# A 3x3 convolution with 2x2 max pooling: the load of the weights is issued by ScalarE instead of SyncE

## The chip, the core and the metric

The kernel runs on one core of a Trainium2 chip. The metric is the device time of one execution in microseconds (us). The kernel before takes 101.24 us, the median of three runs (100.98 to 101.30).

## What is computed

The reference, cut to its core:

```python
# x: (16, 64, 64, 64) f32, weight: (128, 64, 3, 3) f32, zero padding of 1
conv[b, co] += weight[co, ci, kh, kw] * x_pad[b, ci, kh:kh+h, kw:kw+w]   # over ci, kh, kw
output[b, c, i, j] = max(conv[b, c, 2*i:2*i+2, 2*j:2*j+2])               # 2x2 max pooling
```

## The kernel before

**Tiling.** Two images are worked on together: their 2 x 64 input channels fill the 128 partitions, so there are 8 pairs p. A pair is cut into 4 strips of 16 rows, which makes 32 strips s. A strip has two halves h, one for each image, and each half is a matmul stream with 64 rows of the array (two streams, one in each half of the array, run beside each other). The input of pair p stands as bf16 in `xb[p]`. Matmuls (L248, in `product`) read `xb` or sums and differences of its rows (`sum`, `dif`, `skip`, made by `rows_op`, L278) and add up in the eight PSUM banks `acc`. ScalarE takes results out of the banks (L287, L293, L295, L309), VectorE makes the two maxima (L300, L322), and stores to DRAM go out on SyncE's queue (L317).

**The weights.** They are loaded once, as 128 partitions (output channels) x 576 floats, into the tile `wraw` (L105, L106). Nothing can be multiplied before they have been through a chain. ScalarE and VectorE make seven bf16 blocks `wq` out of them: G0, G1, G2 are the three kernel rows (cast on ScalarE, L173), D0, D2, GM and GP are differences and sums of these (on VectorE, L181, by way of `gsum`), and each block gets a copy of its first column group behind its last one (L141, L143). TensorE turns each block with three transposes (L155), and ScalarE and VectorE bring the turned blocks out of PSUM into `wt` (L165, L169), which L248 uses as its weights.

**The first rows.** `HEAD_LOADS` (L39) names six loads of f32 rows into `xf`, issued right behind the weights' load by the loop at L107 through `load` (L89): of pair 0 the rows 0 to 17 (the upper bound is not included), 17 to 33, 33 to 49 and 49 to 64, and of pair 1 the rows 0 to 17 and 17 to 33. They are cast to `xb` by VectorE or ScalarE (L100, in `cast_rows`). All later rows are loaded and cast by GpSimd's DMA queue (L94, in `cload`); the first of them waits for the cast of rows 49 to 64 of pair 0.

**What sets the order.** The schedule is manual. The string `ORDER` lists the work as tokens, and each engine works in the order of its own tokens: `D0`, `GS`, `D2`, `GM`, `GP` are VectorE's weight blocks, `g0a`, `g1a`, `g2a` ScalarE's, `u...` the copies of a column group, `T...` the transposes, `V...` the copies out of PSUM, `CV.p.lo.hi` and `CA.p.lo.hi` the casts of rows on VectorE and ScalarE, `S`, `E`, `D` the sums, differences and skips of rows. SyncE's and ScalarE's DMA issues stand in the order of the code. Ahead of `ORDER`, eight matmuls of ones (L393) keep TensorE at work while the weights come.

Of the kernel before, what the change touches and what calls it, by code (L numbers as in the profile page):

```python
# [10 lines left out]
def kernel(  # L11
# [7 lines left out]
    nc = tc.nc  # L19
# [83 lines left out]
        made_by[f"C.{p}.{lo}.{hi}"] = inst  # L103

    wraw = const.tile([CO, CI * K * K], FP32)  # L105
    nc.sync.dma_start(out=wraw, in_=weight.rearrange("a b c d -> a (b c d)"))  # L106
    for rows in HEAD_LOADS:  # L107
        load(*rows)
    ident = const.tile([128, 128], BF16)
# [358 lines left out]
```

## Time and profile before

| | |
|---|---|
| median of three runs | 101.24 us |
| the profiled execution, its own time | 101.24 us |
| its span (first to last instruction) | 99.4 us |
| busy: TensorE matmuls | 94.3 us (95%) |
| busy: VectorE | 88.0 us (88%) |
| busy: ScalarE | 87.8 us (88%) |
| busy: GpSimd | 58.5 us (59%) |
| moved by DMA | 18.81 MB |

Times in the views count from the start of the span. PE is TensorE's matmuls, PEld its weight loads, DVE is VectorE, ACT ScalarE, POOL GpSimd and SP SyncE; a q behind a name is that engine's instruction queue, on which it issues DMAs. The DMA queue q1 is that of SyncE, q10 that of ScalarE and q0 that of GpSimd. An arrow in square brackets names what the engine was waiting for.

### The profile page before, as it was taken

What the parts mean: (1) busy time and instruction counts of PE and PEld (TensorE: products, weight loads), DVE (VectorE), ACT (ScalarE), POOL (GpSimd) and SP (SyncE); (2) the same over time, 40 slices, a digit from 0 to 9 for tenths busy, and PEclk for the clock granted to TensorE, in tenths of its full rate; (3) what the DMA queues carried; (4) which work ended last, traced back from release to release, by engine and by line L of the source; (5) the groups of instructions that cost most, each with busy time, mean ns of one, the idle gap of its engine ahead of it and who ended that gap; (6) DMA issues with size and microseconds to landing.
All of it is one profiled execution on the core that took longest, in us unless ns stands there. A gap on an engine that the chain in (4) does not pass through costs nothing.

```text
span 99.4 us, 2421 instructions
## 1 busy us (share of the span) xinstructions
PE 94.3 (95%) x857; PEld 63.5 (64%) x857; DVE 88.0 (88%) x178; ACT 87.8 (88%) x196; POOL 58.5 (59%) x55
## 2 busy tenths in 40 slices
PE   6999999999999999999999999999999999999930
PEld 2368445577678755566677777777777777746400
DVE  0599999999999999999999889989989998967970
ACT  5599998999999998998987999999989899999850
POOL 7000897299957947299179998774594399300000
PEclk9999999999999999999999999999999999999999
DMA  2999769999999999999995057898943107333144
GB/s 44 287 352 412 309 86 196 198 160 298 226 217 226 231 231 226 251 255 294 238 308 170 6 178 242 106 220 102 250 163 127 53 7 254 115 113 102 38 141 138
DMA packets 11740, 18.81 MB, mean 189 GB/s; under 512 B 976, under 2 KB 9168, under 8 KB 11728
## 3 DMA queue, kind: packets, MB, share of 16 engines
q0 software_dynamic: 1872, 6.80, 37.5%
q1 hardware_dynamic: 9712, 11.73, 35.7%
q8 instruction: 6, 0.10, 0.4%
q10 hardware_dynamic: 144, 0.13, 0.4%
q14 instruction: 6, 0.05, 0.2%
HBM read 17.07 MB, written 8.39 MB: 256 GB/s over the span
## 4 chain that ended last, share of the span: by engine, by line
PE 82%; DVE 6%; DMA 6%; SPq 1%; issue 0%; ACT 0%; DVEq 0%
PE acc L248 82%; DMA xf<-in_x_dram 6%; DVE acc L300 3%; DVE xb L100 1%; DVE xf L322 1%; DVE skip L278 1%; DVE dif L278 0%; SPq L89 0%; ACT od L309 0%; SPq L106 0%; DVE sum L278 0%; DVEq L463 0%; DVEq L300 0%
## 5 line engine op out<-in xcount | busy, mean ns | idle before, releaser
L248 PE MATMUL acc<-skip,wt_G 64*128 64x504 bf16 (+1 forms) x312 | 64.2, 377 | 0.1
L248 PEld LDWEIGHTS <-wt_G 64*128 64x128 bf16 x432 | 36.8, 94 | 16.3 <-issue 2.0
L300 DVE TENSOR_TENSOR acc<-acc,ev 128x512 f32<-128x512 f32 x64 | 43.1, 693 | 3.0 <-ACT ev L293 1.2
L278 POOL TENSOR_TENSOR skip<-xb 128x1024 bf16<-128x1024 bf16 x18 | 38.0, 2126 | 11.5 <-PE acc L248 2.8
L248 PE MATMUL acc<-dif,wt_GM 64*128 64x512 bf16 (+1 forms) x156 | 39.9, 376 | 0.0
L248 PE MATMUL acc<-sum,wt_GP 64*128 64x512 bf16 (+1 forms) x156 | 37.2, 377 | 0.2 <-DVE acc L300 0.2
L287 ACT COPY acc<-acc 128x512 f32<-128x512 f32 x52 | 30.5, 586 | 2.8 <-PE acc L248 0.9
L293 ACT ACTIVATE ev<-acc 128x512 f32<-128x512 f32 x52 | 31.5, 610 | 1.3 <-PE acc L248 1.0
L309 ACT COPY od<-acc 128x256 f32<-128x256 f32 x64 | 23.0, 382 | 1.5 <-PE acc L248 1.2
L248 PE MATMUL acc<-xb,wt_G 64*128 64x504 bf16 (+7 forms) x84 | 17.5, 340 | 0.0
L248 PEld LDWEIGHTS <-wt_GP 64*128 64x128 bf16 x156 | 14.2, 94 | 5.1 <-issue 0.6
L248 PE MATMUL acc<-xb,wt_D 64*128 64x504 bf16 (+3 forms) x84 | 17.3, 346 | 0.0
L248 PEld LDWEIGHTS <-wt_GM 64*128 64x128 bf16 x156 | 14.4, 94 | 3.8 <-issue 0.5
L322 DVE TENSOR_TENSOR xf<-acc,od 128x256 f32<-128x256 f32 x32 | 12.7, 417 | 1.1 <-ACT od L309 1.0
L278 POOL TENSOR_TENSOR sum<-xb 128x512 bf16<-128x512 bf16 x6 | 6.9, 1150 | 10.9 <-DVE skip L278 7.9
L322 DVE TENSOR_TENSOR o<-acc,od 128x256 f32<-128x256 f32 x32 | 12.7, 416 | 0.6 <-ACT od L309 0.2
L248 PE MATMUL acc<-sum,wt_G 64*128 64x504 bf16 (+1 forms) x36 | 9.6, 377 | 0.0
L278 DVE TENSOR_TENSOR sum<-xb 128x1024 bf16<-128x1024 bf16 (+1 forms) x16 | 9.3, 589 | 0.0
L248 PEld LDWEIGHTS <-wt_D 64*128 64x128 bf16 x84 | 7.0, 94 | 2.0
L94 POOL DMA_DIRECT2D xb<-in_x_dram x13 | 7.8, 602 | 0.0
L278 DVE TENSOR_TENSOR dif<-xb 128x1024 bf16<-128x1024 bf16 (+1 forms) x12 | 7.7, 644 | 0.0
L295 ACT COPY ev<-acc 128x512 f32<-128x512 f32 x12 | 7.1, 604 | 0.0
(38 smaller groups left out, 36.9 us busy)
## 6 DMA issues: line engine op xcount, KB each, us to landing
out_dram<-o SPq DMA_DIRECT2D x15, 256.0 KB, 6.9
xb<-in_x_dram POOLq DMA_DIRECT2D x7, 496.0 KB, 9.3
xb<-in_x_dram POOLq DMA_DIRECT2D x6, 528.0 KB, 8.0
out_dram<-xf SPq DMA_DIRECT2D x8, 256.0 KB, 6.8
out_dram<-xf SPq DMA_DIRECT2D x15, 128.0 KB, 1.9
xf<-in_x_dram SPq DMA_DIRECT2D x3, 512.0 KB, 6.7
xf<-in_x_dram SPq DMA_DIRECT2D x2, 544.0 KB, 6.7
xf<-in_x_dram SPq DMA_DIRECT2D x1, 480.0 KB, 7.4
```

The lines of the kernel that those rows point to most:

```text
L94: inst = nc.gpsimd.dma_start(out=xb[p][:, lo + 1 : hi + 1, :], in_=rows_of(p, lo, hi))
L100: inst = nc.scalar.copy(out=dst, in_=src) if engine == "A" else nc.vector.tensor_copy(out=dst, in_=src)
L248: nc.tensor.matmul(t[:, i0:i1, o0:o1], wt[block][lo : lo + CI, tap_of(block, kw, h), :], rows(lo, i0, i1, c0, c1), start=start and kw == 1 ...
L278: inst = engine.tensor_tensor(out=dst, in0=in0, in1=in1, op=op)
L287: nc.scalar.copy(out=acc[home("B", part, s, h)][:, span, :], in_=acc[home("A", part, s, h)][:, span, :])
L293: nc.scalar.mul(dst, src, -1.0)
L295: nc.scalar.copy(out=dst, in_=src)
L300: nc.vector.tensor_tensor(out=t, in0=t, in1=ev[s % NEV, h][:, span, :], op=MAX)
L309: nc.scalar.copy(out=od[s % NEV, h][:, span, :], in_=acc[home("B", part, s, h)][:, span, 1::2])
L322: nc.vector.tensor_tensor(out=ot[s % len(ot)][:, h, i0:i1, :], in0=t[:, :, 0::2], in1=od[s % NEV, h][:, i0:i1, :], op=MAX)
```

## The change

The load of the weights is issued by ScalarE. Nothing else is changed in the code:

```diff
     wraw = const.tile([CO, CI * K * K], FP32)
-    nc.sync.dma_start(out=wraw, in_=weight.rearrange("a b c d -> a (b c d)"))
+    nc.scalar.dma_start(out=wraw, in_=weight.rearrange("a b c d -> a (b c d)"))
     for rows in HEAD_LOADS:
         load(*rows)
```

Two engines have another program by it. On SyncE, at the start of the program, the rows before, and behind them the rows now, are these (`wraw` is the tile of the weights, `xf_79` and `xf_80` the f32 rows of pairs 0 and 1):

```order
0 L463 UNCONDITIONAL_BRANCH
1 L106 DMA wraw<-in_weight_dram 128x576
2 L89 DMA xf_79<-in_x_dram 128x1088
3 L89 DMA xf_79<-in_x_dram 128x1024 x2
4 L89 DMA xf_79<-in_x_dram 128x960
5 L89 DMA xf_80<-in_x_dram 128x1088
6 L89 DMA xf_80<-in_x_dram 128x1024
```

```order
0 L463 UNCONDITIONAL_BRANCH
1 L89 DMA xf_79<-in_x_dram 128x1088
2 L89 DMA xf_79<-in_x_dram 128x1024 x2
3 L89 DMA xf_79<-in_x_dram 128x960
4 L89 DMA xf_80<-in_x_dram 128x1088
5 L89 DMA xf_80<-in_x_dram 128x1024
6 L317 DMA out_dram<-o_113 128x2x256
```

The weights' load has left SyncE's queue, and each of the six row loads has moved up one place; the load of rows 0 to 17 is now the first.

On ScalarE, also at the start, the program now begins like this:

```order
0 L463 UNCONDITIONAL_BRANCH
1 L106 DMA wraw<-in_weight_dram 128x576
2 L173 ACT_TABLE_LOAD
3 L173 CAST wq_G_142<-wraw 128x192
4 L141 COPY wq_G_142<-wq_G_142 128x64
5 L173 CAST wq_G_144<-wraw 128x192
6 L173 CAST wq_G_143<-wraw 128x192
```

The weights' load stands ahead of the table load, which was the first instruction before; the rest of ScalarE's 199 instructions follow in the same order, and the programs of TensorE, VectorE and GpSimd are the same as before.

## The prediction

> **What bounds the kernel now.** I read the chain of waits first, in order of time, because it names what the end hangs on:
>
> ```profile
> 0.74 0.37 SPq L106
> 1.11 0.06 issue
> 1.17 0.42 SPq L89
> 1.59 0.05 issue
> 1.64 5.93 DMA xf<-in_x_dram
> 7.57 0.02 issue
> 7.59 0.70 DVE xb L100
> ...
> 9.69 0.61 DVE skip L278
> 10.30 0.05 issue
> 10.35 81.31 PE acc L248 x744
> ```
>
> From 10.35 us on TensorE works through 744 matmuls in 81.31 us without a break that the chain would put down to anything else. Whatever moves the point 10.35 moves the end by as much, unless that long run has slack in it, and the chain shows none. So the question is what sets 10.35. The chain says: the landing of rows 17 to 33 at 7.57 (the second load of rows), and behind it VectorE. The change touches two instructions of this chain, the issues at 0.74 and at 1.17, and read by itself it promises rows 0.42 us earlier.
>
> But a chain shows only what ended last, not by how much. So I looked at VectorE's own rows before 7.59:
>
> ```profile
> 3.65 0.50 DVE L181 TENSOR_TENSOR wq_D<-wraw 128x192 bf16<-128x192 f32 x1 [3.65 <-DMA wraw<-in_weight_dram]
> 4.07 0.50 DVE L181 TENSOR_TENSOR gsum<-wraw 128x192 f32<-128x192 f32 x1
> ...
> 5.61 0.50 DVE L181 TENSOR_TENSOR wq_GP<-gsum,wraw 128x192 bf16<-128x192 f32 x1
> 6.03 0.35 DVE L169 COPY wt_D<-acc 128x384 bf16<-128x384 bf16 x1
> 6.29 0.45 DVE L100 CAST xb<-xf 128x576 bf16<-128x576 f32 x1
> 6.66 0.35 DVE L169 COPY wt_G<-acc 128x384 bf16<-128x384 bf16 x1
> 7.04 0.42 DVE L278 TENSOR_TENSOR sum<-xb 128x512 bf16<-128x512 bf16 x1
> 7.59 0.69 DVE L100 CAST xb<-xf 128x1024 bf16<-128x1024 f32 x1
> ```
>
> VectorE starts at 3.65, when the weights have landed, and from there each row starts before the one ahead of it has ended (the first at 3.65 lasts 0.50 and the next starts at 4.07), until 7.04 + 0.42 = 7.46. Only from 7.46 to 7.59 does it stand still for the rows: **0.13 us**. So there are two paths that reach 7.59 nearly together. One is the rows. The other is the weights' landing and 3.81 us of VectorE behind it (7.46 - 3.65). Rows that come earlier are worth 0.13 us at most. Weights that come later cost all of their delay but 0.13 us.
>
> The DMA issues, looked at in the first 3 and the first 2 us, and the use of the DMA engines between the landings:
>
> ```profile
> q1 hardware_dynamic: 129, 0.30, 43.8%
> ...
> wraw<-in_weight_dram SPq DMA_DIRECT2D x1, 288.0 KB, 2.9
> ```
>
> ```profile
> xf<-in_x_dram SPq DMA_DIRECT2D x1, 544.0 KB, 5.1
> xf<-in_x_dram SPq DMA_DIRECT2D x1, 512.0 KB, 5.9
> ```
>
> ```profile
> 0.74:1.74 1.00, 0.96 (x3) 0.43 (x4) 0.00 (x0) 1.00 (x1) 0.93 (x6) 1.00 0.00 0
> 1.74:3.63 1.89, 1.89 (x6) 0.59 (x4) 0.00 (x0) 0.28 (x1) 0.74 (x6) 1.00 1.02 276
> 3.63:6.25 2.62, 2.61 (x22) 1.22 (x20) 2.60 (x9) 2.42 (x8) 0.00 (x0) 1.00 0.99 297
> 6.25:7.57 1.32, 1.21 (x20) 0.98 (x21) 1.18 (x4) 1.32 (x5) 0.00 (x0) 1.00 0.96 338
> 7.57:8.85 1.28, 1.28 (x28) 1.15 (x24) 1.22 (x3) 1.28 (x4) 0.00 (x0) 1.00 0.99 402
> ```
>
> The last two columns are the busy share of the 16 DMA engines and GB/s. The weights land 2.9 us after their issue at 0.74, at 3.64. Rows 0 to 17 land 5.1 us after theirs at 1.17, at 6.27. Nothing moves until 1.74, and from there to 8.85 the DMA engines are busy all the time (0.96 to 1.02). So the queue is no place where an earlier issue finds idle DMA engines: the first packet moved 1.0 us after the first issue, and the rows that were issued second were already standing behind the weights when these were through. The 129 packets of 0.30 MB are 2.3 KB each, one per partition (576 floats of 4 bytes are 2304 bytes).
>
> **The change, step by step.**
>
> SyncE loses one issue of 0.37 us, and its six row loads are issued 1.17 - 0.74 = 0.43 us earlier. Nothing else is affected on that queue: its next work is the first store. On ScalarE the issue comes ahead of the table load. Its price is the nearest row, the store that ScalarE issues at the end:
>
> ```profile
> 0.74 1.28 ACT L173 ACT_TABLE_LOAD   x1 [0.74 <-PEq L449]
> 3.65 0.54 ACT L173 CAST wq_G<-wraw 128x192 bf16<-128x192 f32 x1 [1.63 <-DMA wraw<-in_weight_dram]
> ...
> 96.18 0.38 ACTq L317 DMA_DIRECT2D out_dram<-xf  x1
> ```
>
> The table load then ends at 0.74 + 0.38 + 1.28 = 2.40 instead of 2.02, and ScalarE waits 1.63 us for the weights anyway: cost nothing. That cover is gone only if the issue took over 1.6 us.
>
> **The weights.** Both engines now issue at 0.74: SyncE rows 0 to 17 on q1, ScalarE the weights on q10. Before, both stood on q1, and the weights went first. Two queues on the same DMA engines must share them, and how they do is seen later in this trace, where GpSimd's loads (q0) and the stores (q1) run together, from 29 to 40 us:
>
> ```profile
> DMA packets 1105, 2.52 MB, mean 229 GB/s; under 512 B 94, under 2 KB 622, under 8 KB 1105
> ## 3 DMA queue, kind: packets, MB, share of 16 engines
> q0 software_dynamic: 546, 1.98, 89.2%
> q1 hardware_dynamic: 559, 0.54, 17.6%
> ```
>
> 546 packets of one and 559 of the other: **one for one**, though q0's are nearly four times as large. If that holds here, each of the 8 weight packets of a DMA engine (128 partitions over 16 engines) waits for one row packet, 7 in all before the last. So the weights no longer go first, they end nearly with rows 0 to 17. The price of 7 of 8 row packets has no row of its own; three rows bound it:
> - on the DMA engine that is last, all 8 took from 3.65 to 6.27, that is 2.62 us; 7/8 of it are 2.29 us;
> - at the mean rate of 3.63 to 6.25 (297 GB/s), the load of 128 x 1088 floats, 0.557 MB, takes 1.88 us; 7/8 are 1.64 us;
> - at the best rate in the windows (402 GB/s) it takes 1.39 us; 7/8 are 1.21 us.
>
> The third is the lower end, since at these first addresses no window reached that rate. All 8 row packets ahead of the last of the weights, 2.62 us, is the upper end. I take the middle of the first two, 1.97 us, because the last engine decides, but which one it is will not be the same for both loads. The weights then land at 3.65 + 1.97 = 5.62.
>
> [...]
>
> **Behind the weights.** VectorE's 3.81 us of work follow, then the cast that stood at 7.59: 5.62 + 3.81 = 9.43. Rows 17 to 33 have landed long before: the DMA engines move the same bytes in the same time, so at about 7.57. The wait of 0.13 us is gone, and the shift is 9.43 - 7.59 = **+1.84 us**. ScalarE's casts and TensorE's transposes start from the same landing and shift by 1.97 us, so they cannot hold it back or make it worse. What is late next is everything: the start of TensorE's long run moves from 10.35 to 12.19. GpSimd's first load waits for the cast of rows 49 to 64, which moves along, so its later loads keep their distance to their users.
>
> **The sum.** The profiled execution took 101.24 us, 99.4 of span and 1.84 around it, and is the median itself. 101.24 + 1.97 - 0.13 = 103.08: **103.1 us**. The bounds are 101.24 + 1.21 - 0.13 = 102.3 and 101.24 + 2.62 - 0.13 = 103.7.
>
> **The rivals.**
>
> *Weights first after all (not slower).* If the DMA engines take ScalarE's queue to its end before they turn to SyncE's, or ScalarE's packets are there clearly before SyncE's, the weights land at 3.65 as before, and the rows come right behind them. Then only the wait at 7.59 can shrink: 101.24 - 0.13 = 101.1 us. It decides from the point where row packets ahead of the weights cost less than 0.13 us; a single one costs 0.33 us (2.62/8). For it speaks that both issues come at 0.74; against it the one-for-one count.
>
> *Rows first.* The rows' load goes through whole, then the weights: 2.62 us, 103.7 us. The same sign, within the bounds.
>
> *The clock falls.* The eight fillers, and matmuls of the same 512 columns later:
>
> ```profile
> 0.78 3.57 PE L393 MATMUL acc<-const-bfloat16-1.0 128*128 128x512 bf16 x8 [0.78 <-PEq L449]
> 4.25 0.51 PE L155 MATMUL acc<-ident,wq_G 128*128 128x128 bf16 x3
> ...
> 10.35 0.39 PE L248 MATMUL acc<-skip,wt_G 64*128 64x512 bf16 x1
> 10.57 0.38 PE L248 MATMUL acc<-skip,wt_G 64*128 64x504 bf16 x1
> ```
>
> A filler takes 0.45 us (3.57/8), a later matmul of one stream 0.22 (10.35 to 10.57), so the fillers run at half pace and everything after at the full one. Now the fillers end at 4.35 and the transposes follow at once; with weights at 5.62 TensorE stands still for nearly two microseconds, and the products move from 6.79 to 8.8. If this sent it back to half pace for as long as the fillers had it, it would lose 3.57/2 = 1.8 us more: 103.1 + 1.8 = 104.9 us. Against it: the granted clock is 1.00 in every window of this trace, and no gap of the kind stands in it. [...]
>
> *The delay is absorbed.* If the 744 matmuls held slack, part of the 1.84 us would come back, down to some 101.6 us. The chain speaks against it.
>
> **How the numbers follow.** Forecast 0.70, rows first 0.07, weights first 0.13, clock 0.07, absorbed 0.03. The range takes in the bounds, absorption, and ScalarE's issue being 0.42 us late on top of the upper bound (103.7 + 0.4): 101.6 to 104.1; it leaves out weights first and the clock, 0.20. About 0.3% (0.3 us) is what a measurement of this kernel tells from no change. Weights first gives 0.13 us and so counts as no change, but for a little: faster 0.03, same 0.11. Slower 0.86.
>
> **What would show it.** The first row of VectorE: it starts at about 5.6 if the weights share, at 3.65 if they go first. The row cast that stood at 7.59 has no wait ahead of it, and the chain of waits now begins with `wraw`, not `xf`. The DMA share from 1.74 on is near 1 as before, and rows 17 to 33 land near 7.6. TensorE's unbroken run begins near 12.2 and is about 81.3 us long. I am wrong if VectorE starts before 4.5, if that run gets shorter, or if the granted clock falls below 1.

## The result, and the profile after

The changed kernel takes **104.95 us** (median of four, 104.15 to 105.48) against 101.27 us (four, 100.98 to 101.32). The ratio is 1.0357, with a 95% interval of 1.0321 to 1.0393: slower, as forecast, but 0.85 us above the range. The profiled execution took 104.15 us, with a span of 102.4 us and a mean granted clock of 0.983; it was the fastest of the four. Two runs below, 105.11 us of the rows first again and 103.77 us of the rows held back, lie more than 1.5% above the fastest run of their kernel and are in no median or ratio.

The chain of waits of the changed kernel, its beginning (start, duration, what):

```profile
0.74 5.59 DMA wraw<-in_weight_dram
6.33 0.02 issue
6.36 0.54 ACT wq_G L173
...
6.94 2.59 PE acc L155 x21
9.54 3.10 PE acc L248 x40
...
12.72 0.58 ACT acc L287
13.30 0.04 issue
13.34 81.20 PE acc L248 x744
```

The chain begins with the weights now, which land at 6.33 instead of 3.64. The unbroken run is as long as before (81.20 against 81.31 us) and begins at 13.34 instead of 10.35, 2.99 us later; the span is 3.0 us longer. Everything happened ahead of that run. What is new is that TensorE itself stands in the chain between the weights and the run, where VectorE stood before.

VectorE's rows of the changed kernel:

```profile
6.36 0.50 DVE L181 TENSOR_TENSOR wq_D<-wraw 128x192 bf16<-128x192 f32 x1 [6.36 <-DMA wraw<-in_weight_dram]
...
9.74 0.42 DVE L278 TENSOR_TENSOR sum<-xb 128x512 bf16<-128x512 bf16 x1
10.09 0.69 DVE L100 CAST xb<-xf 128x1024 bf16<-128x1024 f32 x1
...
12.09 0.68 DVE L278 TENSOR_TENSOR skip<-xb 128x1024 bf16<-128x1024 bf16 x1
13.07 1.30 DVE L300 TENSOR_TENSOR acc<-acc,ev 128x512 f32<-128x512 f32 x2 [0.30 <-PE acc L248]
```

The cast that stood at 7.59 starts at 10.09 without a wait: VectorE is 2.50 us late. The run of TensorE is 2.99 us late, so 0.49 us more were lost on the way, and the last row shows VectorE waiting for TensorE. The windows of TensorE's first 13 us (length; busy time with count of PE, PEld, DVE, ACT, POOL; then granted clock, DMA share, GB/s) show where:

```profile
3.60:7.01 3.41, 0.51 (x3) 0.07 (x2) 0.66 (x2) 0.62 (x2) 0.00 (x0) 1.00 1.02 375
7.01:10.42 3.41, 3.41 (x31) 2.62 (x33) 3.37 (x12) 3.27 (x11) 0.00 (x0) 0.50 1.01 408
10.42:13.34 2.92, 2.88 (x49) 2.48 (x45) 2.59 (x6) 2.52 (x7) 0.48 (x1) 1.00 0.37 152
```

The granted clock was 1.00 from 3.60 to 7.01, then for 3.41 us **0.50**, then 1.00 again. The first twelve products, which take 0.83 us in the kernel before, show it:

```profile
9.49 1.27 PE L248 MATMUL acc<-xb,wt_D 64*128 64x256 bf16 x12
```

In the stretch ahead of the drop TensorE was busy for 0.51 of 3.41 us, since it stood still between the fillers and the first transposes:

```profile
0.78 3.27 PE L393 MATMUL acc<-const-bfloat16-1.0 128*128 128x512 bf16 x8 [0.78 <-PEq L449]
6.94 0.56 PE L155 MATMUL acc<-ident,wq_G 128*128 128x128 bf16 x3 [2.90 <-ACT wq_G L173]
```

That leaves the landing of the weights. The packets on SyncE's queue (q1, rows) and on ScalarE's (q10, weights) in the changed kernel, from 2.58 to 4.60 us, and a rate in the stretch ahead of it:

```profile
q1 hardware_dynamic: 87, 0.38, 61.4%
q10 hardware_dynamic: 86, 0.20, 30.2%
```

```profile
1.74:2.58 0.84, 0.84 (x4) 0.29 (x2) 0.00 (x0) 0.71 (x1) 0.74 (x6) 1.00 0.75 130
```

87 to 86: one for one. But until 2.58 us only rows moved (25 packets, the first at 1.75), none of the weights, although both loads were issued at 0.74.

### The profile page after: what moved, and what is told of

Read it like the earlier page. It is cut to its first block, busy times and chain, and to the rows that moved or that the text cites. A ratio compares the mean times of both kernels' runs of the same rounds, so it can differ in the third digit from the quotient of the medians.

```text
span 102.4 us, 2421 instructions
## 1 busy us (share of the span) xinstructions
PE 94.4 (92%) x857; PEld 64.7 (63%) x857; DVE 87.9 (86%) x178; ACT 87.9 (86%) x196; POOL 58.4 (57%) x55
## 4 chain that ended last, share of the span: by engine, by line
PE 85%; DMA 5%; DVE 3%; ACT 1%; issue 0%; DVEq 0%; ACTq 0%
PE acc L248 83%; DMA wraw<-in_weight_dram 5%; PE acc L155 3%; DVE acc L300 3%; DVE xf L322 1%; ACT acc L287 1%; ACT wq_G L173 1%; ACT od L309 0%; DVEq L463 0%; ACTq L287 0%; DVEq L300 0%
## 5 line engine op out<-in xcount | busy, mean ns | idle before, releaser
L248 PE MATMUL acc<-xb,wt_D 64*128 64x504 bf16 (+3 forms) x84 | 17.8, 361 | 0.0
```

Of the source, the lines that this page charges most:

```text
L248: nc.tensor.matmul(t[:, i0:i1, o0:o1], wt[block][lo : lo + CI, tap_of(block, kw, h), :], rows(lo, i0, i1, c0, c1), start=start and kw == 1 ...
```

## The experiments

Three theories were put up. **A**: the weights land late, because their packets are mixed with those of the rows, and the gap that this opens on TensorE lets its clock fall; the time is the sum of both. **B**: the lateness alone costs all of it. **C**: issuing from ScalarE costs something by itself. Ratios are against the kernel before on the same chip. The edits are shown against the changed kernel where nothing else is said, and cut.

**More fillers.** The clock's share alone is taken away: TensorE is kept at work while the weights come.

```diff
-    for n in range(8):
+    for n in range(18):
         nc.tensor.matmul(
-            acc[n].rearrange(...
+            acc[n % 8].rearrange(...
```

> The changed kernel with 18 fillers (L393) instead of 8; nothing else differs. Theory A (late weights plus a clock that falls because TensorE stands still from 4.05 to 6.94 us): the weights still land near 6.3 and VectorE's cast stands near 10.1, but the granted clock is 1.00 between 7 and 10.4 us, the unbroken run of 744 matmuls begins at 10.35 + 2.50 = 12.85 instead of 13.34, and the median falls from 104.95 to 101.27 + 2.5 = 103.8, with a spread of some 0.3 us instead of 1.3. Theory B (the lateness alone costs all, and the clock is only a sign of it): the median stays at 104.5 to 105.5.

Measured: 103.89 us (103.84 to 104.07), ratio 1.0274 (1.0260 to 1.0288), 1.06 us under the changed kernel by the medians and some 0.8 us by the ratios, and the spread shrinks from 1.33 to 0.23 us. The weights landed at 6.61 in the profiled execution, even later than in the changed kernel, and the run still began earlier:

```profile
0.74 5.87 DMA wraw<-in_weight_dram
...
13.18 81.24 PE acc L248 x744
```

```profile
3.64:7.05 3.41, 2.61 (x12) 0.99 (x10) 0.42 (x1) 0.42 (x1) 0.00 (x0) 1.00 1.03 377
7.05:10.47 3.42, 3.12 (x35) 2.12 (x37) 3.38 (x13) 3.24 (x11) 0.00 (x0) 1.00 1.02 413
```

With 2.61 us of work in the stretch, the clock stayed up in the next one (1.00, and three transposes of D in 0.36 and 0.33 us as in the kernel before). B is out as the whole account: nothing but matmuls of ones was added, and the time fell.

**Fewer fillers in the kernel before.** The clock alone, with the weights on time (`range(2)` instead of `range(8)`, in the kernel before):

> The kernel before (weights on SyncE, landing at 3.65 us) with 2 fillers instead of 8, so that TensorE stands still from about 1.6 to 4.25 us; it prices the clock alone. Theory A: the clock rises later than the 4.45 us of before, the transposes and part of the products run at half pace, and the time rises by about the 1.06 us that the fillers gave back in the changed kernel (104.95 against 103.89): 101.8 to 102.8, with a wider spread. Rival (the clock matters only when the weights are late, since VectorE sets the pace up to 10.35): 101.1 to 101.4.

Measured: 102.29 us (101.85 to 103.08), ratio 1.0106 (1.0065 to 1.0147): 1.0 us more, with the weights landing at 3.75. TensorE in this run and in the kernel before, at the same products:

```profile
6.92 1.46 PE L248 MATMUL acc<-xb,wt_D 64*128 64x256 bf16 x12
```

```profile
6.79 0.83 PE L248 MATMUL acc<-xb,wt_D 64*128 64x256 bf16 x12
```

The first row is that of two fillers. Twelve products take 1.46 us instead of 0.83. The granted clock reads 1.00 at that place in this profile, though (4.37 to 9.20), and 1.0 as a mean. So the slow start does not show in the column here; it is read from the pace of the matmuls.

**The order alone, on one queue.** Rows 0 to 17 ahead of the weights, both on SyncE:

```diff
-    nc.scalar.dma_start(out=wraw, in_=weight.rearrange("a b c d -> a (b c d)"))
-    for rows in HEAD_LOADS:
+    load(*HEAD_LOADS[0])
+    nc.sync.dma_start(out=wraw, in_=weight.rearrange("a b c d -> a (b c d)"))
+    for rows in HEAD_LOADS[1:]:
         load(*rows)
```

> Both loads on SyncE's queue, but rows 0 to 17 ahead of the weights; ScalarE issues nothing at the start. Theory A (it is the place of the weights behind or among the first rows that costs): the weights land at 6.0 to 6.4 us as in the changed kernel, the clock falls as there, and the median is 104.3 to 105.5. Theory C (ScalarE's queue costs by itself, by a slow start of it or by ScalarE's own time): the weights land clearly earlier than 6.3, at 5.5 or before, and the median is 103.5 or less.

Measured: 103.83 us (103.59 to 104.60), ratio 1.0280 (1.0244 to 1.0316). The weights landed at 6.13, which speaks for A; the time is below what A gave. So it was run once more beside the changed kernel:

> The changed kernel once more, beside the next one on the same chip. Its four times so far were 104.15 to 105.48 us. If the spread comes from where the clock's fixed stretches of 3.41 us fall against the start of the program, five more times spread alike, 104.1 to 105.6, with a median of 104.4 to 105.2.

> Rows 0 to 17 ahead of the weights on SyncE's queue once more: its median was 103.83, 1.1 us under the changed kernel, though the weights landed only 0.2 us earlier (6.13 against 6.33). If that was the clock's chance in four runs, the two medians of this call lie within 0.5 us of each other. If the change costs something besides the lateness and the clock (ScalarE's issue), this kernel is again 0.7 us or more under the changed one.

Measured: the changed kernel 104.92 us (104.06 to 105.52), ratio 1.0350 (1.0304 to 1.0396); rows first on SyncE 104.21 us (103.34 to 104.83), ratio 1.0271 (1.0222 to 1.0320). The difference is 0.71 us, just above the 0.7 that was set for a cost of ScalarE's issue, though the two intervals overlap; by the ratios it is some 0.8 us here as in the first comparison. The profiled executions landed the weights at 6.33, 6.49 and 6.61 with ScalarE's issue (the last with more fillers) and at 6.13 and 6.06 without, on average 0.4 us later. The other 0.3 to 0.4 us are less than either spread and not explained. So some three quarters of the loss come from the order alone, without any DMA on ScalarE; for the last quarter C is not excluded. It would have to act ahead of the landing, since the stretch from the weights to the long run is not longer with ScalarE's issue (6.98 and 7.69 against 7.57 and 7.32, in the table below).

**The weights alone on ScalarE's queue.** SyncE issues the rows only when the weights have landed (`load` returns its instruction for this):

```diff
-    nc.scalar.dma_start(out=wraw, ...
+    wload = nc.scalar.dma_start(out=wraw, ...
     for rows in HEAD_LOADS:
-        load(*rows)
+        tc.add_manual_dep(load(*rows).ins, wload.ins.name, SYNC, reason="order")
```

> The weights on ScalarE's queue, and SyncE issues the rows only when the weights have landed, so nothing shares with them. If ScalarE's queue starts late by itself, the first packet moves near 2.6 us and the weights land at 4.4 to 4.6. If it was late only because SyncE's load was issued in the same moment, the first packet moves at 1.75 and they land at 3.6 to 3.8. The rows come 1.0 us after their issue, and rows 17 to 33 land 2.5 to 4 us after the weights: the time is 101.8 to 103.0 in the second case, 0.8 more in the first. TensorE's clock does not fall in either.

Measured: the weights land 2.9 us after the issue, at 3.68, as on SyncE. So the weights took no longer on ScalarE's queue here, where nothing was issued beside them.

```profile
0.74 2.94 DMA wraw<-in_weight_dram
3.68 0.02 issue
3.70 4.26 DMA xf<-in_x_dram
```

The time, 104.31 us (104.13 to 105.30), ratio 1.0335 (1.0293 to 1.0376), was not foreseen. The rows landed at 7.96, so the cast ran at 7.98 instead of 6.29, and the clock fell to 0.50 here as well. The transposes came on time (the first at 4.30, against 4.25 before); behind them TensorE waited 1.67 us for rows:

```profile
4.93:8.34 3.41, 1.80 (x18) 1.03 (x16) 1.85 (x7) 1.83 (x7) 0.00 (x0) 1.00 0.91 297
8.34:11.75 3.41, 3.25 (x34) 2.86 (x35) 3.16 (x8) 2.38 (x6) 0.00 (x0) 0.50 1.02 405
```

**Queues swapped.** The weights on SyncE, rows 0 to 17 on ScalarE (`load(*HEAD_LOADS[0], nc.scalar)`, with the engine as an argument of `load`, ahead of the weights on `nc.sync`):

> The weights on SyncE's queue as before, and rows 0 to 17 on ScalarE's queue, both issued at 0.74 us. In the changed kernel ScalarE's first packet moved at 2.58 us, SyncE's at 1.75. If a load on ScalarE's queue starts some 0.8 us later whatever it carries, the rows now start near 2.6 and the weights at 1.75 have most of their 1.2 us behind them by then: they land at 3.7 to 4.3. If the two loads start alike and only share one for one, the weights land at 5.0 to 6.2. Rows 0 to 17 then share with rows 17 to 33, which stand behind the weights on SyncE's queue, and land at 6.3 to 7.4, so the time is 101.5 to 102.5 in the first case and 103 to 105 in the second.

Measured: 104.26 us (103.61 to 104.62), ratio 1.0302 (1.0268 to 1.0337). The weights landed at 5.78. Packets from 1.74 to 2.71 us, and from 2.71 to 4.40 (q1 now begins with the weights, q10 has rows):

```profile
q1 hardware_dynamic: 27, 0.06, 91.9%
```

```profile
q10 hardware_dynamic: 77, 0.34, 58.1%
q1 hardware_dynamic: 86, 0.20, 37.6%
```

Again ScalarE's load started late, now with rows in it. But the head start was worth little, since only 27 packets of the weights moved in it, and the rest was shared about one for one. The forecast of 3.7 to 4.3 for this case fell; at ScalarE's late start the other queue's load was not through.

**Rows held back a little.** The weights on ScalarE as in the changed kernel; SyncE's loads wait for the first zeroing of a border on GpSimd and are issued at 1.48:

```diff
+    zeroed = [nc.gpsimd.memset(t[:, 0 : H + 2 : H + 1, :], 0.0) for t in xb]
+    for rows in HEAD_LOADS:
+        tc.add_manual_dep(load(*rows).ins, zeroed[0].ins.name, SYNC, reason="order")
```

> The changed kernel, with SyncE's row loads held until GpSimd's first zeroing of a border has ended (1.46 us), so that they are issued near 1.5 instead of 0.75 and their first packet moves near 2.5. Theory A (packets are shared one for one from the moment at which both queues have packets): the weights on ScalarE's queue start at 1.75, have more than half of their packets through by 2.5, share the rest, and land at 4.2 to 5.0: 101.6 to 102.6 us. If a head start of 0.75 us is enough for the weights to go through first: landing at 3.6 to 3.8, 101.1 to 101.6. If the whole of the rows still goes ahead of their end: 5.7 or later, over 103.

Measured: 101.80 us (seven runs, 101.49 to 102.84), ratio 1.0064 (1.0027 to 1.0101). Packets up to 2.77 us:

```profile
q10 hardware_dynamic: 115, 0.26, 32.7%
q1 hardware_dynamic: 1, 0.00, 0.4%
```

VectorE started at 3.51: 115 packets had started on q10 when the first row packet moved (113 of the weights' 128, and two of under 512 bytes), so a head start of 0.74 us between the issues was enough here to put the weights first. A's numbers for it (4.2 to 5.0) were too pessimistic. Some four fifths of the loss are gone with nothing but a delay of the *rows*. What is left shows in the profiled execution, at 102.84 us the slowest of the seven: the rows are late now. VectorE's casts wait for them at 7.29 (1.07 us) and at 8.82 (0.46 us), and ScalarE's cast of rows 49 to 64 stands at 11.92 instead of 10.18. TensorE's transposes also ran at a slower pace there (three of D took 0.52 and 0.53 us, against 0.36 and 0.33 before).

**Smaller row packets.** `HEAD_LOADS` begins with (0, 0, 9), (0, 9, 17) instead of (0, 0, 17); the same bytes, in packets about half as large:

> The changed kernel with the load of rows 0 to 17 cut into two, rows 0 to 9 and 9 to 17, so that a row packet is about half as large (2304 and 2048 bytes instead of 4352) while the bytes are the same. Theory A (one packet of the weights for one of the rows): while the 8 weight packets of a DMA engine go, 8 half packets of rows go with them instead of 8 whole ones, so the weights land about 1.0 us earlier than the 6.33 of the changed kernel, at 5.1 to 5.6, and the time falls by 0.7 to 1.2 to 103.8 to 104.2. If the sharing is by bytes, or if the rows go through whole before the weights, they land at 6.0 to 6.6 and the time stays at 104.5 to 105.3.

Measured: 104.03 us (103.72 to 104.56), ratio 1.0275 (1.0241 to 1.0309); the weights landed at 5.26, 1.07 us earlier. That fits sharing by packets (forecast 5.1 to 5.6) and not by bytes (6.0 to 6.6). Whole loads in turn would also have moved the landing here, since the rows' load was cut in two; they are ruled out by the counts instead (below). The clock fell here too, to 0.50 from 7.23 to 10.64, after a stretch with 1.68 us of work; the run began at 12.89.

**Both remedies.** The smaller row packets and 14 fillers:

> Both remedies in one: the changed kernel with rows 0 to 17 loaded as 0 to 9 and 9 to 17, and 14 fillers instead of 8. If the two costs are lateness and clock and nothing else, the weights land near 5.26 as with the smaller row packets alone, TensorE keeps its clock, and the time is 101.27 + (5.28 - 3.65) - 0.13 = 102.8, with 102.5 to 103.1 allowed for the landing. If there is a third cost, it stays over 103.3.

Measured: 103.13 us (102.87 to 103.51), ratio 1.0177 (1.0134 to 1.0219), 0.03 us above the span that was allowed. The weights landed at 4.96 and the run began at 11.53. By the two costs it should have begun at 10.35 + (4.99 - 3.65) - 0.15 = 11.54. So up to the run there is no third cost. The 0.3 us by which the time exceeds the sum lie behind it: at the end of the program (L463) SyncE waits 1.7 us for the last stores here, against 1.2 us before and 1.3 in the changed kernel. With the smaller row packets alone the span, too, ends 3.5 us behind the last piece of its chain, against 3.0 in the changed kernel. Why a seventh load at the start does this was not shown.

**A way to be faster than both.** In the kernel before, the second sum between the casts goes to GpSimd (`S.1` becomes `Sg.1`):

> The kernel before, with the sums of strip 1 (the second of the two on VectorE between the casts of rows 17 to 33 and 33 to 49) made by GpSimd, which stands idle until 10.37. VectorE sets the start of the unbroken run at 10.35 in the kernel before, and the sum holds 0.34 us of that path. If VectorE is what bounds it, the run starts at 10.0 and the time is 101.27 - 0.34 = 100.9, unless the cast of rows 33 to 49 then waits for its landing at 8.85 (it would start at 8.66, so 0.19 of the gain would go): 100.9 to 101.1. If something else reaches 10.35 as late, 101.27 as before.

Measured: 102.01 us (101.85 to 102.33), ratio 1.0071 (1.0045 to 1.0096): 0.7% slower instead of faster. GpSimd's sum, and VectorE's cast and skip that ran beside it, in this run:

```profile
8.91 1.68 POOL L278 TENSOR_TENSOR sum<-xb 128x512 bf16<-128x512 bf16 x1 [6.43 <-DVE dif L278]
```

```profile
8.88 0.69 DVE L100 CAST xb<-xf 128x1024 bf16<-128x1024 f32 x1
9.48 1.65 DVE L278 TENSOR_TENSOR skip<-xb 128x1024 bf16<-128x1024 bf16 x1
```

VectorE saved a sum, and its skip took 1.65 us instead of 0.68, until 11.13. The run, whose first matmul reads that skip, began at 11.19 instead of 10.35.

The two costs side by side, from the profiled executions (us):

| kernel | weight work starts | long run starts | between | median |
|---|---|---|---|---|
| before | 3.65 | 10.35 | 6.70 | 101.27 |
| more fillers | 6.63 | 13.18 | **6.55** | 103.89 |
| both remedies | 4.99 | 11.53 | **6.54** | 103.13 |
| changed | 6.36 | 13.34 | 6.98 | 104.95 |
| changed again | 6.51 | 14.20 | 7.69 | 104.92 |
| rows first | 6.15 | 13.72 | 7.57 | 103.83 |
| rows first again | 6.09 | 13.41 | 7.32 | 104.21 |
| queues swapped | 5.80 | 12.83 | 7.03 | 104.26 |
| smaller row packets | 5.28 | 12.89 | 7.61 | 104.03 |
| two fillers | 3.77 | 11.42 | 7.65 | 102.29 |

Where the clock stayed up and the rows were there, it is 6.55 us from the weights to the run, 0.15 less than before, since the wait for the rows is gone. Where the matmuls ran slower it is 7.0 to 7.7. The changed kernel stands twice in the table, and its two profiles differ in how long TensorE ran at half pace (the 40 products in the chain took 3.10 us in the first and 3.81 in the second): against 6.55 the fastest execution lost 0.43 us by it, the one near the median (104.99) 1.14.

## Why the prediction was right and wrong

*What bounds the kernel*: right. The two paths that met at 7.59 were the point; earlier rows were worth 0.13 us (0.15 in the table), and all that was lost came by way of the weights.

*Earlier issues move no rows earlier*: right. Rows 0 to 17, issued 0.43 us earlier, landed 5.4 us after their issue, at about 6.1 instead of 6.27:

```profile
xf<-in_x_dram SPq DMA_DIRECT2D x1, 544.0 KB, 5.4
```

*ScalarE's issue is hidden*: right. It took 0.40 us, and ScalarE waited for the weights for 3.90 us behind its table load:

```profile
0.74 0.40 ACTq L106 DMA_DIRECT2D wraw<-in_weight_dram  x1
1.17 1.28 ACT L173 ACT_TABLE_LOAD   x1 [1.17 <-PEq L449]
6.36 0.53 ACT L173 CAST wq_G<-wraw 128x192 bf16<-128x192 f32 x1 [3.90 <-DMA wraw<-in_weight_dram]
```

*One for one*: right, by the counts and by the smaller row packets. Up to 3.00 us, 1.25 us after the first row packet, these had moved in the changed kernel:

```profile
q1 hardware_dynamic: 40, 0.17, 28.3%
q10 hardware_dynamic: 16, 0.04, 5.3%
```

At the best rate that the prediction found in a window (402 GB/s), the eight row packets of a DMA engine take an estimated 1.39 us, so by this estimate no engine had finished them when the weights' first packets moved. The trace's packet records do not name the engine; chained by their ends and starts, they fall into 16 chains, most of which show rows and weights in turn. (The 129 packets of the first 3 us, which the prediction took for those of the weights, include six of under 512 bytes; its sum does not use them.)

*The price of sharing, 1.97 us*: the first term that failed. The weights started VectorE's work at 6.36, which is 2.71 us later, above even the upper bound of 2.62 for all eight row packets. "Both engines now issue at 0.74" was taken to mean that both queues also start together; ScalarE's first packet moved at 2.58, 0.84 us after SyncE's. So the rows had a head start, and the weights ended behind the whole load of rows 0 to 17 (about 6.1). In the second profile of the changed kernel and with more fillers the weights' work started later still, at 6.51 and 6.63. This fits all eight row packets going ahead of the last weights instead of seven, at the pace of the last DMA engine and not the middle: 2.62 us, in time the rival *rows first* (0.07). What each profile has beyond that (0.09 to 0.36 us) is not explained.

*Nothing behind the weights makes it worse*: wrong. ScalarE's casts and TensorE's transposes were taken to shift by 1.97 us with no more harm; in the changed kernel the transposes and the products behind them stand in the chain of waits, at a granted clock of 0.50 from 7.01 to 10.42.

*The clock*: the second step that failed, and with the first it put the time out of the range. It stood among the rivals with 0.07, at 1.8 us; that it falls was also named as a sign of being wrong. That the granted clock was 1.00 in every window of before said nothing about gaps, as before had none of the kind, and the column reads 1.00 also during the fillers (1.74 to 3.63), which took 0.45 us each against 0.22 for a later matmul of one stream. In the changed kernel the clock fell after a gap of 2.90 us (4.05 to 6.94), and with the weights alone after a stretch in which TensorE was busy for 1.80 of 3.41 us. The size was 1.06 us in the medians, 0.4 to 1.1 in the profiles. As a sum: 101.27 + 2.71 - 0.15 + 1.06 = 104.89, against 104.95. Its last term is the changed kernel's own median less that with more fillers, so the close fit proves little; but the 1.0 us that the two fillers cost in the kernel before gives 104.83. Without the clock the sum is 103.83, within the range.

*Open*: why a load that ScalarE issues in the same moment as SyncE starts later. With nothing issued beside them the weights landed at 3.68 from ScalarE's queue and at 3.64 from SyncE's, so the queue by itself does not explain it; what the two loads share at that point was not shown. Open as well: the 0.3 to 0.4 us by which rows first on SyncE is faster beyond its earlier landing.

## What to carry to other kernels

A queue was also an order here. On SyncE's queue alone the weights landed at 3.64 when they were issued first, and at 6.13 behind rows 0 to 17; on two queues the packets were mixed, 87 to 86 from 2.58 to 4.60 us, and the weights, which are needed first, landed at 6.33, the rows at about 6.1. Before moving a transfer, ask which of the two ends a wait, and what it is worth to have the other earlier (here 0.13 us). And the gap of 2.90 us on TensorE cost more than the wait: the clock was 0.50 for 3.41 us behind it, worth about 1 us here.

## What the runs showed of the hardware

- The clock changed in stretches of 3.41 us whose place against the start of the program differed from run to run (boundaries at 3.60 in the changed kernel, 4.03 in the second run of rows first and 4.93 with the weights alone). TensorE was busy for 0.51 (changed), 1.80 (weights alone) or 1.68 us (smaller row packets) in a stretch, and the clock was 0.50 in the next one; with 2.61 us (more fillers) it stayed at 1.00. Whether the busy time or the longest gap decides (1.67 us with the weights alone to 2.90 in the changed kernel where it fell, 0.97 with more fillers where it stayed) these runs do not tell apart. That the place of the stretches makes the spread of 1.3 us in the changed kernel is an estimate, from its two profiles, which lost 0.43 and 1.14 us, and from the spread with more fillers, 0.2 us.
- VectorE's skip took 1.65 us instead of 0.68, and GpSimd's sum 1.68 instead of the 1.15 of its next one, when the sum ran beside a cast and that skip, all three on `xb`, in the run with the sum on GpSimd.
- In the changed kernel the first 0.84 us of transfers ran at 130 GB/s, with the DMA engines 0.75 busy; from 7.01 to 10.42 it was 408, with 1.01.
